# A chunked RWKV mixer on one core: the diagonal-block inverse moved ahead of the projection of v, state accumulators in two PSUM banks, two masks moved to VectorE

## The chip, the cores and the metric

The kernel runs on one core of one Trainium2 chip, as one launch. The metric is the device time of the whole launch in microseconds (us), as the median of several runs. Five engines work side by side: TensorE (PE: matmuls, and PEld: its weight loads), VectorE (DVE), ScalarE (ACT), GpSimd (POOL) and SyncE (SP, which here only issues DMAs). Matmul results land in PSUM, which has eight banks; everything else lies in SBUF.

## The reference

The program is a small two-part model over 256 tokens of width 1024. The part that the change touches is the "even mixer" of the second block: eight RWKV-7 heads of 64 channels, beside a multi-scale pooling branch.

```
S_t = S_{t-1} (diag(w_t) + a_t b_t^T) + v_t k_t^T ;  y_t = S_t r_t      (per head)
a = -kk,  b = kk * sigmoid(...),  kk = normalised k
y   = groupnorm(y);  bonus = sum(r * k * r_k) * v
o   = concat[(y + bonus) * g,  multiscale_pool(u_pool)] @ w_out
```

After this mixer comes a mixture of experts (32 experts, two per token), then an odd mixer (differential attention and S5 groups), and a second mixture of experts. Each expert has three weight matrices (gate, up, down) of 2 MB or 1 MB pieces, and they are read from HBM.

## The kernel before

`rwkv()` computes the recurrence in four chunks of 64 tokens. Heads are packed in pairs, so there are four pairs `p` and four chunks `b`, sixteen units of 128 partitions by 64. The work runs in these stages, which the prediction names:

- **Projections.** `shifted()` makes k, r and v: per tile of 128 channels, 24 matmuls of 128x256 (high and low parts of weight and input, L1203 to L1205 in the profile of before), then VectorE's `up` (L1208) and its combination (L1210). After r come four matmuls with `selT` (L1287), and VectorE makes the decayed factors: `AR` (a·decay and r·decay, L1295 and L1304), `sq` (the bonus product, L1313), `bb` (L1299) and `kb` (L1301). Then the projection of v; then the bonus product on PE (L1322), the gate product (L1327), transposes of v (L1333), and the pooling projection (L334 to L336, whose weights are split by VectorE in L326) with its small products.
- **Diagonal blocks.** Per pair, `diag()` multiplies `bb` with `AR` (64x128 per unit: the left half gives the matrix to invert, `Lr`, the right half an output factor, `ArbT`). ScalarE evicts `Lr` (L1429). VectorE masks it to 16x16 blocks (L1432 to L1437) and inverts these by forward substitution, 28 small instructions in a chain (L1441, L1443). Transposes and copies give `Tt` and `Tn`. `early` (L1385) are the factors that are scaled across chunks, for the products between different chunks, `offd()`.
- **State and outputs (the R stage).** Per pair: `diag` and `offd` of `kb`, masks (`lk`, L1474; `ark`, L1417), evictions (L1422, L1424), then the products into the accumulators R and Y, which stay open in PSUM. All these products have the helper's line, L1397.
- **Merging.** The 16x16 inverses become 32x32 (`mo1`) and 64x64 (`mo2`): GpSimd masks `Lr` (L1497), PE multiplies, and ScalarE and VectorE evict.
- **Recursion over the four chunks**, group norm, output projection, routing logits.

In PSUM, banks are handed out from named rings: "x" with six buffers and "w" with two. A scheduler orders the instructions of each engine; the code constrains it by `after()` and by priorities. Tiles come from pools, and a pool's space is used again when it is closed.

The weights of the experts come through a ring of eleven slots of 2 MB, w0 to w10, issued in a fixed order on SP's queue and, for two of the first loads, on GpSimd's. A slot may lie over mixer tiles, and its first load then waits until these are no longer read. The functions that the change touches are shown here.

Of the kernel before, what the change touches and what calls it, by code (L numbers as in the profile page):

```python
# [10 lines left out]
F32 = mybir.dt.float32  # L11
# [133 lines left out]
class K:  # L145
# [998 lines left out]
    def rwkv(self, keep):  # L1144
        nc, A, P, sh = self.nc, self.A, self.P, self.sh
        X = lambda shape: self.bank("x", shape, 6)
# [13 lines left out]
        V = keep.tile([128, 16, 64], F32, name="V")  # L1160
        opool = keep.tile([128, 4, T], F32, name="opool", tag="opool")
# [18 lines left out]
                                   gain=P("mix_g0"), bank="x", nb=6)  # L1180
# [118 lines left out]
        nc.vector.tensor_mul(bb, u16(kk), Ei)  # L1299
        with self.after(kkr):  # L1300
            nc.vector.tensor_mul(kb, u16(k), Ei)  # L1301
# [70 lines left out]
        zz, ux, u4, x1 = (whi(n, i) for i, n in enumerate(("zz", "ux", "u4", "x1")))  # L1372
# [5 lines left out]
        Lc, Ld = (zz[:, 512 * i:512 * i + 512].rearrange("p (u t) -> p u t", u=16) for i in range(2))  # L1378
        Ut = ux[:, 0:512].rearrange("p (u t) -> p u t", u=16)
        Uc, Z = (ux[:, 512 + 256 * i:768 + 256 * i].rearrange("p (u t) -> p u t", u=16) for i in range(2))  # L1380
        pd = lko1[:, 768:1024].rearrange("p (a b) -> p a b", a=16)
        Us, X1s = ([a[:, 512 * i:512 * i + 512].rearrange("p (u t) -> p u t", u=8) for i in range(2)] for a in (u4, x1))
# [5 lines left out]
        HS = [slice(64 * h, 64 * h + 64) for h in range(2)]  # L1388
        Lr = wlo("Lr", 3).rearrange("p (a b) -> p a b", a=16)
# [3 lines left out]

        def mm2(o, lhsT, rhs, start=True, stop=True):

            for h in HS:
                r = nc.tensor.matmul(o[h], lhsT[h], rhs[h], start=start, stop=stop, skip_group_check=not (start and stop))  # L1397
            return r
# [15 lines left out]
        def diag_out(dst, q):  # L1414

            d = bass.AP(tensor=dst.tensor, offset=dst.offset, ap=[dst.ap[0], [T + 64, 4], [1, 64]])
            nc.vector.tensor_mul(d, q[:, :, 64:128], mk("incl", 4))  # L1417
# [14 lines left out]
        nc.vector.tensor_mul(Lc, Lr[:, :, 0:32], C("m16")[:, None, 0:32].to_broadcast([128, 16, 32]))  # L1432
# [824 lines left out]
```

## Time and profile before

| | us |
|---|---|
| median of 3 runs (lowest to highest) | 1562.63 (1562.36 to 1564.98) |
| profiled execution, its own time | 1568.15 |
| span of the profiled execution | 1566.5 |
| PE busy in the span | 1281.4 (82%) |
| VectorE, ScalarE, GpSimd busy | 608.2, 403.6, 197.5 |
| moved by DMA | 499.09 MB, 319 GB/s over the span |

The span runs from the first to the last instruction of one execution that the hardware profiler took. It is 1.65 us shorter than that execution's own time, and that own time is 5.5 us above the median of the unprofiled runs, so differences of stages are applied to the median.

### The profile page before, as it was taken

The page shows a single profiled execution, that of the slowest core. Times are in us where ns is not written, and L with a number is a line of the kernel's source. Part 1 is how long each engine was busy: PE and PEld are TensorE (multiplying, and loading weights), DVE is VectorE, ACT ScalarE, POOL GpSimd, SP SyncE. Part 2 cuts the span into 40 slices and gives each one's busy share as a digit, 9 for nine tenths or more (in the row PEclk, how much of TensorE's full clock was granted, in tenths as well). Part 3 has the DMA queues.
Part 4 walks back from the last instruction along what each step waited for, and adds up shares of the span by engine and source line. Part 5 has one row for each costly group of instructions (what it writes and reads, how often), then busy time and mean ns, then how long its engine had stood idle before and what let it go on. Part 6 is the DMA issues. An engine that isn't in the chain of part 4 may idle for free.

```text
span 1566.5 us, 32856 instructions
## 1 busy us (share of the span) xinstructions
PE 1281.4 (82%) x14522; PEld 929.6 (59%) x14522; DVE 608.2 (39%) x1433; ACT 403.6 (26%) x767; POOL 197.5 (13%) x294
## 2 busy tenths in 40 slices
PE   7999999999978788677678686987888666777786
PEld 6887788779877755453454433866755442643543
DVE  7687678779644312412011012867311000101011
ACT  5455545555432110010010011635110000000011
POOL 2200021000022000742442001023100000000000
PEclk9999999999999898688898799998899897999898
DMA  9544344454307899999999998478899999999996
GB/s 361 191 179 158 141 168 152 158 194 149 150 27 307 360 425 417 410 424 421 419 419 425 425 411 367 127 159 336 337 425 423 426 426 427 423 425 426 424 424 275
DMA packets 51372, 499.09 MB, mean 319 GB/s; under 512 B 9452, under 2 KB 16784, under 8 KB 20632
## 3 DMA queue, kind: packets, MB, share of 16 engines
q1 hardware_dynamic: 50648, 492.20, 77.7%
q0 software_dynamic: 288, 4.19, 0.6%
q8 instruction: 117, 1.92, 0.5%
q10 hardware_dynamic: 288, 0.52, 0.1%
q14 instruction: 31, 0.25, 0.0%
HBM read 494.86 MB, written 2.04 MB: 317 GB/s over the span
## 4 chain that ended last, share of the span: by engine, by line
DMA 33%; PE 14%; DVE 3%; issue 1%; ACT 1%; SPq 0%; ACTq 0%
DMA w<-in_moe_w_down_dram 17%; DMA w<-in_moe_w_up_dram 11%; PE mm L934 4%; PE mm L854 3%; DMA w<-in_moe_w_gate_dram 3%; DMA w<-in_odd_in_dram 2%; PE tp L843 1%; DMA w<-s5H 1%; PE pj L334 1%; PE pj L335 1%; PE pj L336 1%; PE acc L875 0%; SPq L1849 0%; DVE probs L2041 0%; DVE zq L2003 0%
## 5 line engine op out<-in xcount | busy, mean ns | idle before, releaser
L854 PE MATMUL mm<-w,xt 128*32 128x128 f32 x8192 | 302.3, 300 | 114.1 <-DMA w<-in_moe_w_up_dram 49.7
L854 PEld LDWEIGHTS mm<-w,xt 128*32 128x32 f32 x8192 | 255.5, 120 | 155.9 <-issue 86.7
L934 PE MATMUL mm<-w,hidT 128*32 128x512 f32 x896 | 194.0, 663 | 49.7 <-DMA w<-in_moe_w_down_dram 49.1
L858 DVE SCALAR_TENSOR_TENSOR hid<-hid,mm 128x128 f32<-128x128 f32 x64 | 18.3, 286 | 377.0 <-ACT hid L857 377.0
L326 DVE TENSOR_TENSOR wlo<-w,whi 128x1024 fp32r<-128x1024 f32 x116 | 143.2, 1238 | 48.5 <-ACT whi L325 47.6
L325 ACT ACTIVATE whi<-w 128x1024 fp32r<-128x1024 f32 x124 | 131.0, 1058 | 117.9 <-PE pj L336 88.9
L934 PEld LDWEIGHTS mm<-w,hidT 128*32 128x32 f32 x896 | 43.4, 118 | 161.0 <-issue 114.3
L334 PE MATMUL pj<-whi,hT 128*128 128x512 f32 x316 | 123.0, 402 | 11.3 <-ACT whi L325 9.6
L335 PE MATMUL pj<-wlo,hT 128*128 128x512 f32 x316 | 125.5, 401 | 0.0
L336 PE MATMUL pj<-whi,hT 128*128 128x512 f32 x316 | 122.9, 397 | 0.7 <-DVE hT L306 0.7
L868 DVE SCALAR_TENSOR_TENSOR y<-mm,slotsc,y 128x512 fp32r<-128x512 f32 x36 | 26.9, 750 | 192.7 <-ACT y L867 190.0
L867 ACT ACTIVATE y<-mm,slotsc 128x512 fp32r<-128x512 f32 x36 | 24.8, 688 | 271.2 <-PE mm L934 245.3
L857 ACT ACTIVATE hid<-mm 128x128 f32<-128x128 f32 x64 | 17.7, 277 | 277.8 <-PE mm L854 277.8
L843 PEld LDWEIGHTS tp<-ohs,x 128*128 128x128 f32 x512 | 67.2, 215 | 25.3 <-issue 18.3
L843 PE MATMUL tp<-ohs,x 128*128 128x128 f32 x512 | 70.5, 301 | 11.1 <-DVE ohs L795 11.1
L334 PEld LDWEIGHTS pj<-whi,hT 128*128 128x128 f32 x316 | 60.1, 191 | 24.9 <-ACT whi L325 9.6
L336 PEld LDWEIGHTS pj<-whi,hT 128*128 128x128 f32 x316 | 60.0, 190 | 13.5 <-DVE hT L306 1.1
L335 PEld LDWEIGHTS pj<-wlo,hT 128*128 128x128 f32 x316 | 60.1, 190 | 13.0 <-DVE wlo L326 0.8
L875 PE MATMUL acc<-y,ohT 128*128 128x512 f32 x144 | 49.0, 442 | 11.3 <-DVE y L868 5.6
L844 DVE TENSOR_TENSOR xt<-tp,pk 128x512 f32<-128x512 f32 x32 | 22.1, 691 | 87.6 <-PE tp L843 87.6
L862 ACT ACTIVATE hidT<-tp 128x128 f32<-128x128 f32 x64 | 17.7, 277 | 145.6 <-PE tp L861 145.6
L861 PE MATMUL tp<-pk,hid 128*128 128x128 f32 x64 | 21.9, 342 | 31.9 <-DVE hid L859 31.4
(715 smaller groups left out, 2001.1 us busy)
## 6 DMA issues: line engine op xcount, KB each, us to landing
w<-in_moe_w_gate_dram SPq DMA_DIRECT2D x64, 2048.0 KB, 30.5
w<-in_moe_w_up_dram SPq DMA_DIRECT2D x64, 2048.0 KB, 22.4
w<-in_moe_w_down_dram SPq DMA_DIRECT2D x54, 2048.0 KB, 27.7
w<-in_w_in_dram SPq DMA_DIRECT2D x14, 2048.0 KB, 7.8
w<-in_moe_w_down_dram SPq DMA_DIRECT2D x16, 1024.0 KB, 30.3
w<-in_w_out_dram SPq DMA_DIRECT2D x4, 2048.0 KB, 7.8
w<-in_w_ple_gate_dram SPq DMA_DIRECT2D x4, 2048.0 KB, 7.8
w<-in_even_in_dram SPq DMA_DIRECT2D x4, 2048.0 KB, 8.0
```

The costliest lines, as they stand in the source:

```text
L325: nc.scalar.activation(h, w[:, i:i + s], AF.Copy)
L326: (engine or nc.vector).tensor_sub(l, w[:, i:i + s], h.bitcast(F32))
L334: nc.tensor.matmul(out, ah, wh, start=start, stop=False)
L335: nc.tensor.matmul(out, ah, wl, start=False, stop=False)
L336: return nc.tensor.matmul(out, al, wh, start=False, stop=stop)
L843: nc.tensor.matmul(p[:, k], xk[t][:, 4 * h + k], ohs[:, t], start=t == 0, stop=t == 1)
L844: nc.vector.tensor_mul(xt[:, ks], p, R["g"][:, ks, None].to_broadcast([128, 4, 128]))
L854: nc.tensor.matmul(gu[32 * q:32 * q + 32, i], xt(k), w[:, k, 128 * q:128 * q + 128], start=k == 0, stop=k == 7)
L867: nc.scalar.activation(y[0][b][r], dn[r], AF.Copy, scale=sc[r, 0:1])
L868: nc.vector.scalar_tensor_tensor(y[1][b][r], dn[r], sc[r, 0:1], y[0][b][r].bitcast(F32), op0=ALU.mult, op1=ALU.subtract)
L875: self.nc.tensor.matmul(acc[t][b], ohT[r, t], y[i][b][r], start=start and i == 0, stop=stop and i == 1)
L934: nc.tensor.matmul(dn[32 * j:32 * j + 32], hT[j][:, k], wd[j][:, 4 * b + k], start=k == 0, stop=k == 3)
```

## The change

1. The "x" ring has four buffers, and a new ring "q" has two, used for `offd` of `kb` and the first half of the output projection.
2. The matrix to invert, `Lr`, is made by 32 small products (64x64) of `bb` with the left half of `AR`, right after `bb` and ahead of the projection of v in the code. The masks and the forward substitution follow there too. `Lr`, `zz`, `ux` and `pd` get tiles of their own in the pool `keep`; before they lay in tiles shared with weight halves. `Tn` moves to the pool `rw_main`.
3. The right halves (`ArbT`) are 64x64 products of their own, in the "w" ring, later, beside `offd` of `bb`.
4. The accumulators R lie in two banks of eight units instead of four banks of four.
5. The masks of `mo1` and `mo2` are made by VectorE, into two tiles, `u4` and `u5`, instead of by GpSimd into one tile used twice.

```diff
-        X = lambda shape: self.bank("x", shape, 6)
+        X = lambda shape: self.bank("x", shape, 4)
+        Q = lambda shape: self.bank("q", shape, 2)
...
+        for i in range(2):
+            q = X([128, 8, 64])
+            for u in range(8 * i, 8 * i + 8):
+                mm2(q[:, u % 8], bb[:, u], ar[:, u, 0])
+            nc.scalar.activation(Lr[:, 8 * i:8 * i + 8], q, AF.Copy)
+        nc.vector.tensor_mul(Lc, Lr[:, :, 0:32], C("m16")[:, None, 0:32].to_broadcast([128, 16, 32]))
...
+        for t in range(2, 16):
+            nc.vector.tensor_mul(pd[:, 0:t, 0:t], Z[:, 0:t, 0:t],
+                                 Uc[:, t, 0:t][:, None, :].to_broadcast([128, t, t]))
+            nc.vector.tensor_reduce(Z[:, 0:t, t], pd[:, 0:t, 0:t], axis=AX.X, op=ALU.add)
         with self.after(kkr):
             nc.vector.tensor_mul(kb, u16(k), Ei)
...
-        for p in range(4):
-            q = diag(p, bb, X)
-            us = slice(4 * p, 4 * p + 4)
-            nc.scalar.activation(Lr[:, us], q[:, :, 0:64], AF.Copy)
-            diag_out(ArbT[:, p], q)
...
+        for U, us in zip(Us, (slice(0, 8), slice(8, 16))):
+            nc.vector.tensor_mul(U, Lr[:, us], mk("mo1", 8))
         Tt = m.tile([128, 16, 64], F32, name="Tt", tag="Tt")
-        Tn = keep.tile([128, 16, 64], F32, name="Tn", tag="Tn")
+        Tn = m.tile([128, 16, 64], F32, name="Tn", tag="Tn")
...
         for p in range(4):
             offd_out(ArbT[:, p], LabO[:, p], offd(p, bb, X))
+            q = W([128, 4, 64])
+            for b in range(4):
+                mm2(q[:, b], bb[:, 4 * p + b], AR0[:, p, b, 1])
+            diag_out(ArbT[:, p], q)
...
-        Rb = [[X([128, 4, 64]) for _ in range(2)] for _ in range(2)]
-        R = lambda b, p: Rb[p // 2][b // 2][:, 2 * (b % 2) + p % 2]
+        Rb = [X([128, 8, 64]) for _ in range(2)]
+        R = lambda b, p: Rb[p // 2][:, 2 * b + p % 2]
...
-            offd_out(Ark, LkO, offd(p, kb))
+            offd_out(Ark, LkO, offd(p, kb, Q))
...
+        for U, us in zip(U2s, U8):
+            nc.vector.tensor_mul(U, Lr[:, us], mk("mo2", 8))
         for n in ("mo1", "mo2"):
-            for U, us in zip(Us, U8):
-                nc.gpsimd.tensor_mul(U, Lr[:, us], mk(n, 8))
-            for U, X1, us in zip(Us, X1s, U8):
+            for U, X1, us in zip(Us if n == "mo1" else U2s, X1s, U8):
                 prod(X1, U, Tn[:, us])
...
-        bk = ("x", [128, 512], 6)
-        op = self.out_proj(oT, [[bk, bk], [bk, bk]], split)
+        bk = [(n, [128, 512], k) for n, k in (("q", 2), ("x", 4))]
+        op = self.out_proj(oT, [[bk[0]] * 2, [bk[1]] * 2], split)
```

The scheduler turns this into another order on the engines. Lines of the changed kernel are 4 higher than before up to the new code, and 10 to 33 higher behind it; the helper of small products is L1309 there.

On PE, behind the projection of r, the kernel before goes from the four `selT` products straight into the projection of v (L1203 to L1205, 96 products):

```order
L1278 MATMUL w<-pk,kkn_y 8x128 x2
L1287 MATMUL x<-kkr,selT 128x256 x4
L1203 MATMUL x<-hT,whi 128x256 x2
L1204 MATMUL x<-hT,wlo 128x256
L1205 MATMUL x<-hT,whi 128x256
L1203 MATMUL x<-hT,whi 128x256
```

The changed kernel has this there:

```order
L1282 MATMUL w<-pk,kkn_y 8x128 x2
L1291 MATMUL x<-kkr,selT 128x256 x4
L1355 MATMUL w<-srk,sq 128x8 x8
L1360 MATMUL w<-w_2840,lr 128x512
L1309 MATMUL x<-AR_2930,bb 64x64 x32
L1207 MATMUL x<-hT,whi 128x256
```

The bonus product (L1322 before, L1355 now), which stood behind the projection of v, the first gate product (L1360) and the 32 new small products now stand ahead of it.

On VectorE, at the same place, the kernel before mixes the work for v and for the pooling weights into the factors:

```order
L1313 TENSOR_TENSOR sq<-r,k 128x1024
L1295 SCALAR_TENSOR_TENSOR AR_2930<-kk,Eg 128x16x64
L1208 TENSOR_TENSOR up_3012<-x,rstdb 128x256
L326 TENSOR_TENSOR wlo<-w_3625,whi 128x1024
L1208 TENSOR_TENSOR up_3013<-x,rstdb 128x256
L1298 TENSOR_TENSOR kk<-kk,ta 128x1024
L326 TENSOR_TENSOR wlo<-w_3625,whi 128x1024
L1210 SCALAR_TENSOR_TENSOR V<-up_3012,evc,V 128x256
L1210 SCALAR_TENSOR_TENSOR V<-up_3013,evc,V 128x256
L1299 TENSOR_TENSOR bb<-kk,G 128x1024
```

The changed kernel has the factors first, then the masks, and then the substitution (L1330, L1332):

```order
L1346 TENSOR_TENSOR sq<-r,k 128x1024
L1299 SCALAR_TENSOR_TENSOR AR_2930<-kk,Eg 128x16x64
L1302 TENSOR_TENSOR kk<-kk,ta 128x1024
L1357 COPY bon<-w 128x8
L1303 TENSOR_TENSOR bb<-kk,G 128x1024
L1357 COPY bon<-w 128x8
L1363 TENSOR_TENSOR P_2922<-w,w_2840 128x512
L1321 TENSOR_TENSOR zz<-Lr,evc 128x512
```

The two `up` instructions, the two weight splits and the two V instructions that stood between sq and bb now stand behind the masks, between the steps of the substitution; `bon` (L1357), which needs the bonus product, stands ahead of bb.

On PE, at the start of the R stage, the kernel before has one pair's products up to the first wait (`lk` and `early` are the masked and evicted products of `kb`):

```order
L1397 MATMUL w<-AR_2930,kb 64x128 x4
L1397 MATMUL w<-early,kb 64x384 x2
L1397 MATMUL x<-V,lk 64x64 x2
L1397 MATMUL w<-early,kb 64x256 x2
L1397 MATMUL w<-early,kb 64x128 x2
L1397 MATMUL x<-V,early 64x64 x2
```

The changed kernel has there:

```order
L1309 MATMUL w<-AR_2930,kb 64x128 x8
L1309 MATMUL q<-early,kb 64x384 x2
L1309 MATMUL q<-early,kb 64x256 x2
L1309 MATMUL w<-AR_2930,kb 64x128 x8
L1309 MATMUL q<-early,kb 64x128
L1309 MATMUL x<-V,lk 64x64 x2
```

The `offd` products of `kb` (64x384, 64x256, 64x128) go to the ring q, and those of the first two pairs' `diag` (64x128 x8, twice) stand ahead of the first product into R; the `offd` of the first pair stands earlier still, among the pooling products.

## Rows read from the trace of the kernel before

**Rows 1.** Windows of the span, with clock, DMA share and rate.

```profile
core 0: us, PE busy (x) PEld busy (x) DVE busy (x) ACT busy (x) POOL busy (x), PEclk, DMA share, GB/s
524.00:532.00 8.00, 8.00 (x190) 7.83 (x193) 2.38 (x7) 0.66 (x2) 0.00 (x0) 0.91 0.37 113
...
532.00:960.00 428.00, 321.93 (x5000) 201.19 (x4991) 73.99 (x273) 37.87 (x102) 97.42 (x224) 0.87 1.01 420
```

**Rows 2.** Timeline of SP's queue of weight loads, 405 to 536 us.

```profile
479.47 0.33 SPq L244 DMA_DIRECT2D w<-in_moe_w_gate_dram  x1
...
531.51 0.33 SPq L244 DMA_DIRECT2D w<-in_moe_w_gate_dram  x1
```

**Rows 3.** Waits of SP's queue, 400 to 560 us.

```profile
SPq L244 <- PE x L1397: 56.9, 1, 56.9
...
SPq L244 <- PE mm L854: 21.7, 8, 6.9
```

**Rows 4.** Timeline of PE around the projections.

```profile
365.20 0.48 PE L1239 MATMUL x<-lr,w 64*128 64x256 f32 x1 [0.51 <-ACT ld L1240]
...
380.62 2.35 PE L1287 MATMUL x<-kkr,selT 8*128 8x256 f32 x8 [0.62 <-DVE kkr L1280]
...
397.15 1.84 PE L1322 MATMUL w<-srk,sq 128*128 128x8 f32 x16
...
411.24 1.02 PE L1327 MATMUL w<-w,lr 128*128 128x512 f32 x2
```

**Rows 5.** Windows: v at either clock, then the R stage.

```profile
382.97:388.83 5.86, 5.86 (x28) 5.86 (x29) 5.86 (x9) 0.19 (x1) 0.00 (x0) 0.50 0.30 78
388.83:397.15 8.32, 8.32 (x70) 8.32 (x70) 8.32 (x11) 3.90 (x5) 0.00 (x0) 0.99 0.47 199
...
428.20:456.80 28.60, 23.18 (x380) 19.65 (x378) 14.94 (x47) 11.55 (x33) 0.66 (x1) 0.88 0.18 74
```

**Rows 6.** Timeline of VectorE, factors, masks and inverse.

```profile
389.02 1.21 DVE L1313 TENSOR_TENSOR sq<-r,k 128x1024 f32<-128x1024 f32 x1
...
396.16 1.21 DVE L1299 TENSOR_TENSOR bb<-kk,G 128x1024 f32<-128x1024 f32 x1
...
411.44 3.50 DVE L1385 TENSOR_TENSOR early<-AR,E 128x1536 f32<-128x1536 f32 x3 [2.22 <-PE x L336]
...
423.37 1.52 DVE L1432 TENSOR_TENSOR zz<-Lr,evc 128x512 f32<-128x512 f32 x1
424.81 0.68 DVE L1433 TENSOR_TENSOR zz<-Lr,evc 128x512 f32<-128x512 f32 x1
...
428.05 0.16 DVE L1441 TENSOR_TENSOR lko<-ux 128x4 f32<-128x4 f32 x1
...
436.83 0.42 DVE L1474 TENSOR_TENSOR lk<-w,evc 128x256 f32<-128x256 f32 x1 [1.32 <-PE w L1397]
...
437.92 0.39 DVE L1443 TENSOR_REDUCE ux<-lko 128x15 f32<-128x225 f32 x1
```

**Rows 7.** Timeline of PE, small products of the chunk stages.

```profile
415.31 1.53 PE L1397 MATMUL x<-AR,bb 64*64 64x128 f32 x24
...
423.63 4.09 PE L1397 MATMUL x<-early,bb 64*64 64x256 f32 x36
...
428.32 0.98 PE L1397 MATMUL x<-evc,V 64*64 64x64 f32 x27
...
432.15 0.33 PE L1397 MATMUL x<-V,lk 64*64 64x64 f32 x4 [1.59 <-DVE lk L1474]
...
443.15 0.33 PE L1397 MATMUL x<-V,lko 64*64 64x64 f32 x4 [3.56 <-ACT lko L1422]
...
458.23 2.08 PE L1397 MATMUL w<-x,Tt 64*64 64x64 f32 x64
```

**Rows 8.** Waits of PE, 411 to 480 us.

```profile
PE w L1397 <- POOL u L1497: 2.1, 1, 2.1
```

**Rows 9.** Timeline of GpSimd, one mask.

```profile
423.07 1.26 POOL L1497 TENSOR_TENSOR u<-Lr,evc 128x512 f32<-128x512 f32 x1 [1.67 <-ACT Lr L1429]
```

More of the change, by code (lines that the diff above doesn't have):

```diff
@@ L1160, in rwkv @@
         V = keep.tile([128, 16, 64], F32, name="V")
+        Lr = keep.tile([128, 16, 64], F32, name="Lr")
+        zz, ux = (keep.tile([128, 1024], F32, name=n) for n in ("zz", "ux"))
+        pd = keep.tile([128, 16, 16], F32, name="pd")
         opool = keep.tile([128, 4, T], F32, name="opool", tag="opool")
@@ L1299, in rwkv, with mm2 @@
         nc.vector.tensor_mul(bb, u16(kk), Ei)
+        HS = [slice(64 * h, 64 * h + 64) for h in range(2)]
+        def mm2(o, lhsT, rhs, start=True, stop=True):
+            for h in HS:
+                r = nc.tensor.matmul(o[h], lhsT[h], rhs[h], start=start, stop=stop, skip_group_check=not (start and stop))
+            return r
+        Lc, Ld = (zz[:, 512 * i:512 * i + 512].rearrange("p (u t) -> p u t", u=16) for i in range(2))
+        Ut = ux[:, 0:512].rearrange("p (u t) -> p u t", u=16)
+        Uc, Z = (ux[:, 512 + 256 * i:768 + 256 * i].rearrange("p (u t) -> p u t", u=16) for i in range(2))
+        for i in range(2):
[4 more added lines that the diff above has]
+        nc.vector.tensor_mul(Lc, Lr[:, :, 0:32], C("m16")[:, None, 0:32].to_broadcast([128, 16, 32]))
+        nc.vector.tensor_mul(Ld, Lr[:, :, 32:64], C("m16")[:, None, 32:64].to_broadcast([128, 16, 32]))
+        nc.vector.tensor_add(Lc, Lc, Ld)
+        nc.vector.transpose(Ut.rearrange("p t c -> p (t c)"),
+                            Lc.rearrange("p u (i t) -> p t u i", i=2))
+        nc.vector.tensor_add(Uc, Ut[:, :, 0:16], Ut[:, :, 16:32])
+        nc.gpsimd.tensor_copy(Z, C("eye16").rearrange("p (x t) -> p x t", x=16))
+        nc.vector.tensor_copy(Z[:, 0:1, 1], Uc[:, 1, 0:1])
+        for t in range(2, 16):
+            nc.vector.tensor_mul(pd[:, 0:t, 0:t], Z[:, 0:t, 0:t],
+                                 Uc[:, t, 0:t][:, None, :].to_broadcast([128, t, t]))
+            nc.vector.tensor_reduce(Z[:, 0:t, t], pd[:, 0:t, 0:t], axis=AX.X, op=ALU.add)
         with self.after(kkr):
@@ L1371, in rwkv @@
         wlo = lambda n, i, dt=F32: sh.tile([128, 1024], dt, name=n, tag=f"wlo{i}")
-        zz, ux, u4, x1 = (whi(n, i) for i, n in enumerate(("zz", "ux", "u4", "x1")))
+        u4, x1 = whi("u4", 2), whi("x1", 3)
+        u5 = wlo("u5", 3)
         lk_, lko1 = wlo("lk", 0), wlo("lko1", 1)
@@ L1377, in rwkv @@
         ark1 = wlo("ark", 2)
[L1378 to L1382, printed above, removed]
+        Us, U2s, X1s = ([a[:, 512 * i:512 * i + 512].rearrange("p (u t) -> p u t", u=8) for i in range(2)] for a in (u4, u5, x1))
         for b in range(3):
@@ L1538, in rwkv @@
             for h in range(2):
-                copy(h, Rs[:, hs[h]], Rb[h][b // 2][:, 2 * (b % 2):2 * (b % 2) + 2])
+                copy(h, Rs[:, hs[h]], Rb[h][:, 2 * b:2 * b + 2])
             q = [W([128, 2, 64]) for _ in range(2)]
```

32 lines of the change are left out of this document (7 added, 25 removed).

## The prediction

> **What bounds the kernel now.** I read the windows of the span first. From 532 to 960 us, the first mixture of experts, the sixteen DMA engines are busy all the time, at 420 GB/s, while PE has idle time [rows 1]: the expert weights set the pace there. So I looked for where the stream of weights is held up. It is held up to 479.47 us: SP's next load waits 56.9 us for a product of the mixer (L1397, the recursion), because its slot lies over a mixer tile [rows 2, 3]. From there the ring fills; then all eleven slots are full, and from 524 to 532 us the rate is 113 GB/s [rows 1]. It resumes at 531.51 us, when the first expert's gate products (L854) give a slot back [rows 2, 3]. These products need the routing, the routing needs the mixer's output, and behind 531.51 us the stream is one piece. So whatever the mixer's end gains or loses moves the end of the kernel by the same amount, and the chain through the mixer, 380 to 506 us, is what must be costed. The profiled execution is 1568.15 us with a span of 1566.5; the median is 1562.63, and I apply the shift to the median.
>
> In that chain PE works nearly without a break from 383 to 428 us; the stage behind it, 428.2 to 456.8 us, holds 23.18 us of PE work in 28.6 us at a mean clock of 0.88 [rows 5], with two idle times, 1.59 us for VectorE's mask and 3.56 us for ScalarE's eviction [rows 7]. VectorE spends 428.05 to 438.31 us on the substitution, 28 instructions of 0.16 to 0.39 us [rows 6], on the same queue as those masks. One more PE wait stands further down: 2.1 us for GpSimd's mask [rows 8].
>
> **The change part by part.** I follow it by landmarks, each before against after.
>
> *Four X buffers instead of six.* The trace shows PE waiting 0.51 us for ScalarE's eviction of an X bank with six [rows 4]. With four, such waits come earlier, in the decay and gate products and at the transposes of the input. Nothing shows their size; below nothing is excluded, since no product gets a bank earlier, and above I bound it by one such wait for each of the eight products, 4 us. I take 1.5 us, three such waits. So the products with selT, which end at 382.97 us [rows 4], end at 384.5.
>
> *Start of v.* Before, v follows selT at once. Now PE has the bonus product next, which needs sq. VectorE finishes sq at 390.23 us [rows 6], so after at 391.7: PE stands idle some 7 us. Then bonus (1.84 us at full clock) and gate product (1.02 us) [rows 4] take 2.9 us, or 5.7 at half clock, to 394.6 or 397.4 us. On VectorE bb now comes after AR, kk·ta and the first bon; three instructions of 1.2 us end at about 395.4, where they ended at 397.37 before with splits and v between them [rows 6]. The 32 products of 64x64 have no row of their own form ahead of v; 64 records of a merging product of that form last 2.08 us, 27 of v's centring 0.98 [rows 7], two records to a product, so the 32 take 2.0 to 2.3 us, twice that at half clock. v thus starts between 397.5 and 401 us; I take 399. That is 16 us later than before.
>
> *v and the pooling projection.* Before, the first 5.86 us of v ran at clock 0.50, that is 1.2 GHz, 28 records; the rest made 70 records in 8.32 us at 2.4 GHz [rows 5], 0.119 us each. 96 products at full clock are 11.4 us against 14.2: v ends near 410.5 us, 13.3 later than its 397.15. If the clock is still low at its start, up to 3 us more. Behind it the bonus product (1.84 us) has gone, so that the pooling projection, whose end was at 411.24 us [rows 4], ends near 422.6, 11.4 later.
>
> Here the Trainium skill speaks against the change: "TensorE: Matmul & The Clock Gate", section "HAM oscillation — how this bites in real kernels", says that waits between bursts of matmuls drop the array to half rate, and that the burst behind them begins cold. The trace agrees in kind: the clock was 0.50 in v's first part, behind the light 8-row products. By that rule the new idle time would cost v its first part again, and the sum would end 3 us later than mine. This is the second rival's mechanism below.
>
> *The substitution on VectorE.* ScalarE evicts Lr by about 399.7. The masks, transpose and first column take some 3.9 us, from the masks' start to the first step being 4.7 before, with one mask of 1.52 us that is 0.68 undisturbed [rows 6]. The steps took 10.3 us before, of which 1.32 us was a wait for PE and some 1.4 us four masks of the R stage in between [rows 6]; without these 7.5 us. Between them now stand v's four up and four V instructions (0.4 us each by the mask of the same 128x256 shape) and four splits of 128x1024, 1.13 us from start to start as sq [rows 6], less one up that comes ahead, 7.3 us, and the two mo2 masks, 1.4 us. Behind them three bonus and gate instructions of 128x512, two of the half masks and a transpose, 4.5 us. In sum 399.7 + 3.9 + 7.5 + 7.3 + 1.4 + 4.5 = 424.3 us is where early starts, against 411.44 [rows 6]. Its first third is done 1.75 us later, at 426.05. Early is so bound by VectorE, with PE some 2 us ahead of it. This is 12.9 us later than before.
>
> *Between chunks.* From 426.05 PE has, at rates of before: five offd groups (four of bb and the first of kb; 36 records of one form in 3.9 us, 12 records to a group, 1.35 us each [rows 7]), the rest of the pooling products 0.6 us, the right halves of diag 1.9 us (64 records of half the width; 24 whole ones take 1.46 us to the next row's start [rows 7]), and the centring of v, 1.9 us. Then the first kb groups, diag twice and offd once (0.86 + 1.35 + 0.86 us), stand ahead of the first product into R. It starts near 441 us, against 432.15 [rows 7].
>
> *R stage.* 28.6 us before, of which 5.2 us are the two waits of [rows 7], and by the mean clock of 0.88 (0.24 of the window at 1.2 GHz, 6.9 us [rows 5]) half-speed stretches cost 3.4 us; without them it is 20.0. Now masks and evictions of the first two pairs are ready before their products, no step of the substitution stands before a mask, and 3.1 us of diag and offd are already counted: four times 2.4 us of products into R and Y, and two more diag and offd groups of 2.25 us, 14.1 us, to 455.1. A wait left between, for ScalarE's evictions, would cost at most what one did before, 3.56 us. With mo1's first products partly inside, their end, where the next merging products begin, is near 457 us, where it was 458.23 [rows 7]: 1.2 us earlier.
>
> *Masks.* mo2's products waited 2.1 us for GpSimd [rows 8], one of whose masks takes 1.26 us [rows 9]. VectorE now makes them from Lr long before, at 0.69 us each: 2.1 us less. VectorE's first mask of zz took 1.52 us while that one ran, from 423.07 us, and the second 0.68 [rows 6, 9].
>
> That fits the Trainium skill, "SBUF — State Buffer", section "Who interferes with whom": a VectorE instruction with two SBUF inputs and a GpSimd instruction that reads SBUF hold each other up. By it, 0.8 us go away here, on VectorE alone.
>
> *The rest.* R in two banks changes no product count; the recursion's copies and products now share banks, between 0 and 0.5 us, I take 0.3. The clock may drop in the shorter stage behind R: 0 to 1.7 us (half of one of the two stretches that the 6.9 us make), I take 0.8.
>
> *Two loads earlier.* Lr, zz and pd, and so the end of the first two slots' covers, are free, by the order of the tiles' last readers, at about 459 us (GpSimd's copy of opool, ahead of the merging) and not at 479: two loads of 2 MB, 4.9 us each at 420 GB/s, start ahead of the recursion's end. I cost them at nothing: the ring is full at 524 us and stands until 531.51 us [rows 1, 2]. If the stream were not full there they would be worth up to 9.9 us.
>
> **Sum.** −1.2 (R stage's end, with all the delay ahead of it) −2.1 (mask) +0.3 (recursion) +0.8 (clock) = −2.2 us. 1562.63 − 2.2 = **1560.4 us**. The sum is a small difference of large terms: +13 us up to early, −4 in the products between chunks, −10 in the R stage.
>
> **The rivals.**
> 1. *The gap is hidden better.* If v starts by 397.5 us and VectorE's substitution is ended sooner (its first and last instructions are 0.16 and 0.39 us [rows 6], so a mean near 0.25, 7 us busy, and the rest is gaps that other work can fill), early starts 3.4 us sooner, at 421, PE-bound, and with no clock loss and the X waits at 0.5 us the sum is −2.2 − 3.4 − 0.8 − 1 = −7.4, 1555 us. For it: gaps between dependent steps. Against it: the pooling projection on PE ends only near 422.
> 2. *Slower: v starts cold and late.* PE stands idle 7 us ahead of the bonus product and works in pieces until bb; v's first part again at clock 0.50 costs 3 us, the small products at half clock 2 us more, and from early on the chain takes them one for one: −2.2 + 3 + 2 + 2 (one more wait for an eviction in the R stage) = +4.8, 1567.4 us. It decides from the point at which early's first third comes later than 428.3 us. For it: the clock row of v before [rows 5]. Against: 3 of the 5 us fall on PE while VectorE is behind PE by 2 us there.
> 3. *The two earlier loads count in full*: −2.2 − 9.9 = −12.1, 1550.5 us. Against it the full ring and the idle rate of 113 GB/s behind 524 us [rows 1].
> 4. *It does nothing here*: the chain through the mixer isn't what the stream waits for, and another load holds the first expert: 1562.6 us. Against it the L854 wait [rows 3].
>
> **How the numbers follow.** Forecast 0.48 with a range of its own from 1557 to 1563.6, rival 1 0.17, rival 2 0.20, rival 3 0.06, rival 4 0.09. A change under 0.2%, 3.1 us, is about what a measurement here can't tell from none. Of the forecast, some 0.18 lie more than 3.1 us below, so faster is 0.18 + 0.17 + 0.06 = 0.41; slower is 0.19, nearly all of rival 2; the same 0.40. The range from 1553.5 to 1567.5 leaves out rival 3, and the tails of rivals 1 and 2.
>
> **What would show it.** PE: an idle time of about 7 us ahead of the bonus product, behind selT; v starting near 399 and ending near 410.5; the clock there at 1.00 (right) or 0.50 (rival 2). VectorE: early near 424. PE: first R product near 441, last near 455, no wait above 1 us between them; no wait for GpSimd at mo2. SP: two loads near 459, and the stream resuming some 2 us ahead of 531.5, with the slow stretch behind 520 us still there; if it is gone, rival 3 holds. The prediction is wrong if the loss ahead of early differs from 13 us by more than the R stage can absorb, or if the R stage still waits for ScalarE's evictions.

## The result and the profile after

The changed kernel is slower: a median of 1573.06 us over five runs (1570.08 to 1576.65), beside 1562.72 us of the kernel before over five runs (1562.36 to 1564.98). The ratio is 1.0059, with a 95% interval from 1.0044 to 1.0075. That is +10.3 us by the medians, +9.2 by the ratio, where I had forecast −2.2; it is slower than rival 2, the slowest case that I had priced (1567.4 us).

The profiled execution of the changed kernel took 1576.65 us, 3.6 us above its median. The page of the profile begins so:

```profile
span 1575.0 us, 32979 instructions
...
PE 1284.9 (82%) x14586; PEld 936.9 (59%) x14586; DVE 605.3 (38%) x1437; ACT 403.0 (26%) x765; POOL 191.6 (12%) x290
```

The engines have almost the same busy time as before, so the time went into the order and the waits. The timeline of PE in the changed kernel has the landmarks of the prediction (a row is: start, us, instruction, and in brackets the idle time ahead of it and what released it):

```profile
344.50 0.88 PE L298 MATMUL x<-pk,x 128*128 128x128 f32 x6 [1.85 <-DVE x L638]
...
385.19 2.39 PE L1291 MATMUL x<-kkr,selT 8*128 8x256 f32 x8 [0.62 <-DVE kkr L1284]
...
394.86 3.59 PE L1355 MATMUL w<-srk,sq 128*128 128x8 f32 x16 [7.27 <-DVE sq L1346]
398.30 2.06 PE L1360 MATMUL w<-w,lr 128*128 128x512 f32 x2
400.28 3.62 PE L1309 MATMUL x<-AR,bb 64*64 64x64 f32 x64
403.83 0.39 PE L1207 MATMUL x<-hT,whi 128*128 128x256 f32 x1
...
427.49 0.40 PE L336 MATMUL x<-whi,hT 128*128 128x512 f32 x1
...
446.88 0.22 PE L1309 MATMUL x<-V,lk 64*64 64x64 f32 x1
...
463.26 2.03 PE L1309 MATMUL w<-x,Tt 64*64 64x64 f32 x63
467.15 2.08 PE L1309 MATMUL w<-Tn,u 64*64 64x64 f32 x64
469.07 0.67 PE L1309 MATMUL w<-Tt,x 64*64 64x64 f32 x15
...
472.20 2.83 PE L1309 MATMUL w<-Tt,x 64*64 64x64 f32 x49 [2.46 <-issue]
474.82 0.64 PE L1309 MATMUL w<-rsa,Tt 64*64 64x64 f32 x8
```

The reader sees the idle time of 7.27 us ahead of the bonus product (L1355), as forecast. Behind it the bonus product, the gate product and the 32 small products (two records each) take 9.0 us, from 394.86 to 403.83 without a gap; the bonus product alone took 1.84 us before [rows 4], here 3.59. Then the first R product at 446.88 us, mo1's second products (L1309, x and Tt) at 463.26, and a new wait of 2.46 us in mo2's last products that the profile calls issue: PE waits there for nothing that the profile shows. The wait for GpSimd's mask [rows 8] is gone. VectorE, in the same profile:

```profile
404.59 0.69 DVE L1321 TENSOR_TENSOR zz<-Lr,evc 128x512 f32<-128x512 f32 x1 [2.88 <-ACT Lr L1320]
...
427.93 3.50 DVE L1415 TENSOR_TENSOR early<-AR,E 128x1536 f32<-128x1536 f32 x3
```

Early, which started at 411.44 us before [rows 6], starts at 427.93. The windows of the changed kernel (columns as in rows 1) show the clock:

```profile
390.00:400.00 10.00, 5.14 (x18) 3.92 (x18) 8.59 (x13) 0.00 (x0) 1.90 (x2) 0.50 0.58 212
400.00:411.00 11.00, 11.00 (x124) 10.65 (x124) 6.79 (x16) 4.41 (x6) 0.00 (x0) 0.83 0.01 2
...
440.00:460.00 20.00, 20.00 (x403) 18.23 (x401) 5.57 (x13) 8.84 (x35) 0.00 (x0) 1.00 0.42 178
...
472.20:475.00 2.80, 2.80 (x53) 2.80 (x54) 0.69 (x1) 0.00 (x0) 0.00 (x0) 0.50 0.95 404
```

Behind the idle time the granted clock stays at 0.50, that is 1.2 GHz, until v starts near 404 us; from 404 to 408 us it is 1.00. From 440 to 460 us, with the R stage from 446.88 on, PE has no idle time at all and a clock of 1.00, where before the R stage had 23.18 us of work in 28.6 at 0.88 [rows 5]. The last row is the end of mo2, behind the issue wait: half clock again. On SP's queue of weight loads:

```profile
463.55 0.33 SPq L244 DMA_DIRECT2D w<-in_moe_w_gate_dram  x1
463.97 0.39 SPq L244 DMA_DIRECT2D w<-in_moe_w_up_dram  x1
...
523.38 14.24 SPq L244 DMA_DIRECT2D w<-in_moe_w_down_dram  x2
539.04 0.33 SPq L244 DMA_DIRECT2D w<-in_moe_w_gate_dram  x1
```

Two loads go out at 463.55, and the stream resumes at 539.04 us, 7.5 us later than at 531.51 [rows 2], while the two spans differ by 8.5: most of the loss lies ahead of this point.

**The kernel before, once more.** The profile behind the prediction is of an execution 5.4 us above its kernel's median. The unchanged kernel was profiled once more (e12_before_again, below); that execution took 1563.01 us, close to the median. From here on stages are compared with it. Its timeline of PE, then of VectorE, then of SP:

```profile
379.07 1.99 PE L1287 MATMUL x<-kkr,selT 8*128 8x256 f32 x8 [0.61 <-DVE kkr L1280]
...
427.71 0.33 PE L1397 MATMUL x<-V,lk 64*64 64x64 f32 x4 [1.60 <-DVE lk L1474]
...
453.65 2.08 PE L1397 MATMUL w<-x,Tt 64*64 64x64 f32 x64
...
463.93 0.44 PE L1397 MATMUL w<-rsa,Tt 64*64 64x64 f32 x8
```

```profile
407.00 3.50 DVE L1385 TENSOR_TENSOR early<-AR,E 128x1536 f32<-128x1536 f32 x3 [2.21 <-PE x L336]
```

```profile
526.53 0.33 SPq L244 DMA_DIRECT2D w<-in_moe_w_gate_dram  x1
```

Both timelines are laid on the eight transposes of the input (L298), which start at 340.14 us in this execution and at 340.75 in the changed kernel's. From there, stage by stage (us; the forecast stands against the profile that it was made on):

| stage, by start of its landmarks | before, again | after | difference | forecast difference |
|---|---|---|---|---|
| transposes to selT | 38.9 | 44.4 | +5.5 | +1.5 |
| selT to early | 27.9 | 42.7 | +14.8 | +11.4 |
| early to the first R product | 20.7 | 18.9 | −1.8 | −4.0 |
| first R product to mo1's second products | 25.9 | 16.4 | −9.6 | −10.1 |
| these to the recursion's first product | 10.3 | 11.6 | +1.3 | −1.3 |
| the recursion's first product to the resumed stream | 62.6 | 64.2 | +1.6 | +0.3 |
| sum | | | +11.8 (11.9 before rounding) | −2.2 |

### The profile page after: what moved, and what is told of

Read it like the earlier page. It is cut to its first block, busy times and chain, and to the rows that moved or that the text cites. A ratio compares the mean times of both kernels' runs of the same rounds, so it can differ in the third digit from the quotient of the medians.

```text
span 1575.0 us, 32979 instructions
## 1 busy us (share of the span) xinstructions
PE 1284.9 (82%) x14586; PEld 936.9 (59%) x14586; DVE 605.3 (38%) x1437; ACT 403.0 (26%) x765; POOL 191.6 (12%) x290
## 4 chain that ended last, share of the span: by engine, by line
DMA 31%; PE 16%; DVE 3%; issue 1%; ACT 1%; POOL 0%; SPq 0%; ACTq 0%; POOLq 0%
DMA w<-in_moe_w_up_dram 17%; DMA w<-in_moe_w_down_dram 9%; PE mm L934 4%; PE mm L854 4%; DMA w<-in_moe_w_gate_dram 3%; DMA w<-in_odd_in_dram 2%; PE pj L334 1%; PE pj L335 1%; PE tp L843 1%; PE pj L336 1%; PE mm L957 0%; PE acc L875 0%; DVE probs L2051 0%; PE tp L1975 0%; DVE omx L2053 0%
## 5 line engine op out<-in xcount | busy, mean ns | idle before, releaser
L854 PEld LDWEIGHTS mm<-w,xt 128*32 128x32 f32 x8192 | 258.7, 122 | 146.0 <-issue 72.0
L934 PE MATMUL mm<-w,hidT 128*32 128x512 f32 x896 | 189.1, 654 | 52.0 <-DMA w<-in_moe_w_down_dram 51.2
L334 PE MATMUL pj<-whi,hT 128*128 128x512 f32 x316 | 123.7, 404 | 11.4 <-ACT whi L325 9.7
L843 PEld LDWEIGHTS tp<-ohs,x 128*128 128x128 f32 x512 | 68.8, 219 | 28.6 <-issue 22.1
```

The lines of the kernel that those rows point to most:

```text
L334: nc.tensor.matmul(out, ah, wh, start=start, stop=False)
L843: nc.tensor.matmul(p[:, k], xk[t][:, 4 * h + k], ohs[:, t], start=t == 0, stop=t == 1)
L854: nc.tensor.matmul(gu[32 * q:32 * q + 32, i], xt(k), w[:, k, 128 * q:128 * q + 128], start=k == 0, stop=k == 7)
L934: nc.tensor.matmul(dn[32 * j:32 * j + 32], hT[j][:, k], wd[j][:, 4 * b + k], start=k == 0, stop=k == 3)
```

## The experiments

Three theories stood against each other when I saw the result. **A**: the x ring of four banks is too short, and its waits and the half clock behind them are the loss. **B**: the order is, with v late behind bonus, gate and small products. **C**: the two earlier loads disturb PE. All kernels but e3, e7, e10 and e12 are edits of the changed kernel. Each ratio is against the kernel before, run beside it on the same chip.

**e1_six_banks** gives the projections' products, decay, selT and v the two q banks as well: banks 1 to 4 from x, 5 and 6 from q, in turn.

```diff
+        def X6(shape):
+            i = self.six % 6
+            self.six += 1
+            return X(shape) if i < 4 else Q(shape)
...
-            ps = X([128, T])
+            ps = X6([128, T])
```

> The changed kernel, but the projections of the low-rank inputs, k, r, the decay products, selT and v take their PSUM banks in turn from the four of x and the two of q, as if there were six again; all else as changed. Theory A (the four-bank ring is the cause: PE's waits at the input's transposes and the tanh products drop its clock twice, and v's first bank comes only after the small products): selT some 4 to 5 us earlier than in the changed kernel, v right behind selT near 383 us, no idle time of 7 us, early near 414 instead of 427.9, and a time of 1553 to 1560 us. Rival B (VectorE's chain with the substitution in it is the bound whatever the banks are): early moves by at most the 5 us of selT, and the time is 1566 to 1570 us.

Measured: 1562.38 us, ratio 0.9995 [0.9985, 1.0005]. That is between the numbers of the two theories, nearer A: by the ratios it is 0.64%, or 10.0 us, faster than the changed kernel, so the whole loss is gone, but no gain appears. In its profile selT's products, then early:

```profile
381.38 1.12 PE L1296 MATMUL q<-kkr,selT 8*128 8x256 f32 x4 [0.62 <-DVE kkr L1289]
419.05 3.48 DVE L1420 TENSOR_TENSOR early<-AR,E 128x1536 f32<-128x1536 f32 x3
```

Early comes 8.9 us sooner than in the changed kernel. From selT to early it is 37.7 us, 5.0 less than there: half of v's products now stand ahead of the bonus product. But v waits for its first bank, and the issue wait stayed (waits of PE, of this kernel: us in total, times, longest):

```profile
PE q L1212 <- DVE kk L1297: 4.5, 1, 4.5
...
PE w L1314 <- issue: 2.0, 1, 2.0
```

**e2_late_loads** was to hold the two loads back by two one-column copies on ScalarE that read `zz` and `Lr` behind the recursion.

```diff
+            for i, t in enumerate((zz, Lr[:, 0])):
+                nc.scalar.activation(gn[1][:, i:i + 1], t[:, 0:1], AF.Copy)
```

> The changed kernel, with two one-column copies by ScalarE, of zz and of Lr into a scratch tile, at the end of the recursion, so that the two loads of expert weights over these tiles can't start at 463.5 us but only behind the recursion. Theory C (the two earlier loads hold up PE's instruction fetch: PE waited 2.46 us for issue in the merging, and its clock fell behind that): that wait goes, the recursion starts 2.5 to 4 us earlier, and the time is 1569 to 1571 us against 1573. Rival D (the fetch is late whatever the loads do, or the loads bring what the wait costs): no difference, 1573 us, or up to 5 us slower if the earlier loads count.

Measured: 1572.17 us, 1.0057 [1.0041, 1.0074]. The copies did not hold the loads (they still start at 462.22 and 462.64 us), so the run says nothing on C.

**e3_masks_alone** is the kernel before with nothing but the masks of mo1 and mo2 on VectorE, in a fifth tile.

```diff
+        u5 = m.tile([128, 1024], F32, name="u5")
...
+        for U, us in zip(Us, (slice(0, 8), slice(8, 16))):
+            nc.vector.tensor_mul(U, Lr[:, us], mk("mo1", 8))
...
+        for U, us in zip(U2s, U8):
+            nc.vector.tensor_mul(U, Lr[:, us], mk("mo2", 8))
...
-                nc.gpsimd.tensor_mul(U, Lr[:, us], mk(n, 8))
```

> The kernel before with only one part of the change: the masks of mo1 and mo2 on VectorE, those of mo2 in a tile of their own. If the 2.1 us wait of PE for GpSimd's mask is worth its full size: no such wait, and 1560 to 1561 us against 1562.7. Rival: VectorE's four masks (0.69 us each) stand ahead of the substitution and of the R stage's masks and take back 1 to 3 us: 1562 to 1564 us.

Measured: 1556.92 us, 0.9958 [0.9941, 0.9975], or −6.6 us: three times the 2.1 us that the wait was, and more than either side had expected. The R stage shows the rest; its window, in the kernel before again and then here:

```profile
424.00:440.00 16.00, 10.65 (x156) 8.40 (x154) 12.96 (x40) 6.20 (x16) 0.00 (x0) 0.85 0.29 123
```

```profile
424.00:440.00 16.00, 14.13 (x242) 11.26 (x237) 14.72 (x47) 7.61 (x24) 0.00 (x0) 1.00 0.39 166
```

With the masks in other places the scheduler also moved ScalarE's copies of Tt behind the evictions of `lko`. The wait of 3.6 us for `lko` (as in [rows 7]) is gone, waits of 1.6 us for `early` and 1.3 for `lk` remain, and with shorter idle times the clock stays at 1.00. Laid on the same point, the stream resumes 7.4 us sooner, of which I count 2.1 to the mask's wait and most of the rest to this stage: from the first R product to mo1's second products it takes 21.3 us here, from 428.41 to 449.70, for 25.9.

**e4_v_first** keeps four banks, and puts the small products and the substitution behind the last product of v.

```diff
+        wv_ = load(2)
...
+        for p in range(4):
+            with self.after(kkr):
+                shifted(wv_, p, 8 + p, v[:, p])
...
-                mm2(q[:, u % 8], bb[:, u], ar[:, u, 0])
+            with self.after(self.last_sh):
+                for u in range(8 * i, 8 * i + 8):
+                    mm2(q[:, u % 8], bb[:, u], ar[:, u, 0])
```

> The changed kernel with its four banks, but the 32 small products and the substitution put behind the projection of v on PE. Theory A, its second half (v behind the small products at half clock is a loss of its own): v starts near 388 us, early comes some 5 to 7 us earlier than 427.9, and the time is 1566 to 1569 us; the delay at selT of 5 us stays. Rival B (VectorE's chain from Lr to early is the bound, and Lr comes no sooner here): early near 427, 1572 to 1574 us.

Measured: 1569.01 us, 1.0039 [1.0026, 1.0051]. By the ratios that takes back 0.20%, a third of the loss, and its interval overlaps the changed kernel's; in the profiles the stretch from selT to early is 39.7 us for 42.7. PE's largest wait in this stretch is now v's first product, for a bank:

```profile
PE x L1207 <- DVE kk L1292: 4.5, 1, 4.5
```

The four selT products hold all four banks of the ring until VectorE has read them (kk, L1292); what stands ahead of that read is shown under e7.

**e5_held_loads** holds the loads with two one-column additions on VectorE that read `pd` and `Lr`, and SA of the recursion; nothing uses their result.

```diff
+        for i, t in enumerate((pd[:, 0], Lr[:, 0])):
+            nc.vector.tensor_add(gn[1][:, i:i + 1], t[:, 0:1], SA[:, 0, 0:1])
```

> The changed kernel with two one-column additions by VectorE, of pd and of Lr to the last state of the recursion, into a scratch tile: they need the recursion's last result, so the two loads over pd and Lr can only start behind it, as in the kernel before. (The copies of the run with late loads waited for nothing and held nothing: its loads still started at 462.) Theory C (the two earlier loads hold up PE's instruction fetch): PE's wait for issue of 1.7 to 2.5 us in the merging is gone, and the time is 1569 to 1571 us. Rival D (the wait is there whatever the loads do): the wait stays, 1572 to 1574 us.

Measured: 1568.01 us, 1.0028 [1.0016, 1.0040], 0.31% better than the changed kernel, some 4.8 us. The loads start at 481.82 us, and the merging has no issue wait (one of 0.3 us stands in the R stage). Windows of the merging, in the changed kernel and here:

```profile
460.00:475.00 15.00, 12.54 (x353) 12.29 (x351) 3.75 (x6) 4.41 (x7) 9.29 (x4) 0.90 0.70 280
```

```profile
460.00:475.00 15.00, 14.37 (x413) 13.53 (x411) 5.03 (x9) 6.43 (x12) 11.41 (x5) 1.00 0.01 3
```

So C is real: wait and half clock go with the loads. Every other stage of the table agrees with the changed kernel's within 0.4 us; this one, from mo1's second products to the recursion, takes 7.8 us for 11.6. What the wait is, the DMA queues suggest. Queue q8 carries PE's instructions, judged by its count: 118 packets for PE's 29,172 instructions. From 462.5 to 469.5 us (packets, MB, share of the engines) the changed kernel moves weights alone, and this kernel one packet of instructions:

```profile
q1 hardware_dynamic: 115, 1.88, 72.1%
```

```profile
q8 instruction: 1, 0.02, 1.1%
```

In the changed kernel none comes in these 7 us; over 455 to 482 us it has five, as the kernel before. Its next one falls in 468 to 470 us:

```profile
q8 instruction: 1, 0.02, 3.1%
```

More finely, it starts at 469.8 us, as PE's wait begins, and 8.0 us behind the packet before it; in e5 the same packet comes 4.5 us behind the one before. Counted in the traces, it comes when PE has started 5797 to 5825 instructions (matmuls and weight loads) in the five kernels that have the wait, and 5611 to 5626 in the nine profiles without it; in all five PE goes on 2.2 to 2.4 us after it. So PE stood for instructions that came late. That the weight packets held them up is inferred from the runs without the loads.

**e6_six_banks_v_first** is e1 with v's block, and the two factors that stood ahead of it, ahead of the small products in the code, as in e4, but without e4's constraint; the small products take the six banks too.

```diff
+        wv_ = load(2)
+        v = V.rearrange("p (a b) t -> p a (b t)", a=4)
+        for p in range(4):
+            with self.after(kkr):
+                shifted(wv_, p, 8 + p, v[:, p])
...
-            q = X([128, 8, 64])
+            q = X6([128, 8, 64])
```

> The run with six banks, with the small products and the substitution put behind v in the code, so that v's first bank is not one that selT or the small products hold; there PE waited 4.5 us for it. Theory A: v right behind selT with no wait, early near 413, the R stage without long waits, and 1553 to 1557 us. Rival B (VectorE's chain with the substitution is the bound): early no sooner than 418, 1560 to 1563 us.

Measured: 1560.24 us, 0.9982 [0.9972, 0.9991]. Against e4, also with v first, that is 0.57%, or 8.9 us, which is the price of the short ring and of e4's constraint together. Early starts at 413.95 us, where A had it, but the time is B's; an issue wait of 1.6 us remains.

**e7_four_banks_alone** is the kernel before with the x ring of four and R in two banks; the two banks saved are left unused.

```diff
-        X = lambda shape: self.bank("x", shape, 6)
+        X = lambda shape: self.bank("x", shape, 4)
...
-        Rb = [[X([128, 4, 64]) for _ in range(2)] for _ in range(2)]
-        R = lambda b, p: Rb[p // 2][b // 2][:, 2 * (b % 2) + p % 2]
+        Rb = [X([128, 8, 64]) for _ in range(2)]
+        R = lambda b, p: Rb[p // 2][:, 2 * b + p % 2]
```

> The kernel before with only the accumulators R in two banks and the x ring of four; two PSUM banks stay unused; all work and its order in the code as before. Theory A, first half (four banks for the projections cost 3 to 5 us at selT, and nothing gives it back): selT 3 to 5 us later, and 1565 to 1568 us. Rival: the delay at selT is taken back behind it, since VectorE is the later engine there: 1562 to 1564 us.

Measured: 1575.64 us, 1.0076 [1.0064, 1.0089]: +11.9 us, more than the whole change. Its waits of PE from 340 to 520 us, and windows of PE and all engines at v:

```profile
PE x L1397 <- DVE lk L1474: 4.8, 1, 4.8
PE x L1203 <- DVE kk L1288: 4.5, 1, 4.5
...
PE x L298 <- DVE x L638: 2.3, 2, 1.9
```

```profile
383.00:390.00 7.00, 2.50 (x12) 1.97 (x11) 7.00 (x11) 0.30 (x1) 0.00 (x0) 0.64 0.17 33
390.00:400.00 10.00, 10.00 (x66) 10.00 (x66) 8.75 (x10) 3.03 (x4) 0.00 (x0) 0.74 0.46 188
```

The same first window in the kernel before again is full, at full clock:

```profile
383.00:390.00 7.00, 7.00 (x61) 7.00 (x60) 7.00 (x11) 2.12 (x2) 0.00 (x0) 1.00 0.63 222
```

v's bank costs 4.5 us of waiting, and the clock falls with it. VectorE's timeline of this kernel shows why the bank is late:

```profile
382.18 0.40 DVE L1280 COPY kkr<-w 8x256 f32<-8x256 f32 x1
382.51 1.20 DVE L1301 TENSOR_TENSOR kb<-k,G 128x1024 f32<-128x1024 f32 x1
383.65 4.61 DVE L1073 TENSOR_TENSOR wlo<-w,whi 128x1024 fp32r<-128x1024 f32 x4
388.19 0.47 DVE L1210 SCALAR_TENSOR_TENSOR r<-up,evc,r 128x256 f32<-128x256 f32 x1
388.58 1.40 DVE L1288 TENSOR_TENSOR kk<-kk,x 128x256 f32<-128x256 f32 x4
```

Between the copy that selT waits for and the four kk that read its banks stand `kb`, four weight splits and one `r`, 6.1 us. With six banks two were free for v meanwhile. Early starts at 419.39 us, 11.4 us later by the transposes: the whole loss stands ahead of early, 2.6 us of it ahead of selT. The wait of 4.8 us for `lk` comes in place of the waits that the kernel before has in the R stage, which takes 24.4 us here for 25.9; so R in two banks has no visible part in the loss.

**e8_six_v_held** joins e6 with the held loads of e5 (the two additions shown there).

> The run with six banks and v first, with the two additions that hold the two loads of expert weights back until the recursion's end. Theory C: 2 to 3 us faster than without them, 1551 to 1554 us. Rival D: the same as without them; if the earlier loads bring something, slower.

Measured: 1557.72 us, 0.9962 [0.9950, 0.9973]. No issue wait is left. Against e6 the held loads bring 0.20%, 3.1 us, with intervals that just touch.

**e9_products_later** moves e8's small products behind the first gate product, and masks and substitution with them in the code, since PE waited 1.3 us for `bb` in e8.

```diff
...
+            with self.after(gm0):
+                for u in range(8 * i, 8 * i + 8):
```

> The run with six banks, v first and held loads, with the 32 small products put behind the first gate product on PE. There PE waited 1.3 us for bb, and its clock was low until about 401 us. If that small stall and the clock behind it are worth their size, and the substitution has room behind early: no wait for bb, 1555 to 1556.5 us against 1557.7. Rival: the substitution is late next, and lk or the merging wait for it: 1557 to 1560 us.

Measured: 1558.42 us, 0.9959 [0.9944, 0.9974], no different from e8. The wait for `bb` has gone, another has come, and early starts later (417.24 us):

```profile
PE w L1349 <- DVE bon L1346: 1.7, 1, 1.7
```

**e10_selT_in_q** is e7 with the four selT products in the two unused banks, two to a bank, so that v finds its x banks free.

```diff
-            q = X([128, 2, T])
+            if p % 2 == 0:
+                qs = self.bank("q", [128, 2, T], 2)
```

> The run with four banks alone (1575.6 us), with the four products of selT in two banks of a ring of their own, two to a bank, so that v's first banks don't wait for VectorE's readers of selT. If v's 4.5 us wait and its clock at half speed behind that make most of the 12 us: v behind selT without a wait, and 1566 to 1569 us. Rival (the waits ahead of selT and in the R stage make most of it): 1571 to 1575 us.

Measured: 1569.83 us, 1.0039 [1.0024, 1.0054], 5.8 us better than e7. The windows at v:

```profile
383.00:390.00 7.00, 5.92 (x43) 5.07 (x42) 6.10 (x8) 1.46 (x2) 0.00 (x0) 1.00 0.01 2
390.00:400.00 10.00, 10.00 (x76) 9.07 (x75) 10.00 (x17) 4.21 (x6) 0.00 (x0) 1.00 0.57 210
```

No bank wait and no half clock there, and from selT to early it is 30.2 us, for 36.8 in e7: by the ratios this one wait, with the clock behind it, is about half of what the short ring costs (their intervals allow a quarter to three quarters). What is left stands, in this profile, ahead of selT, 44.5 us from the transposes for 38.9 (3.0 of the 5.6 us are half-clock stretches that e7's execution didn't have), and in the R stage, 28.5 us for 25.9, with waits of 5.5 us for `lko` and 2.0 for `ark`.

**e11_masks_gpsimd** is e8 with the masks on GpSimd again.

```diff
-            nc.vector.tensor_mul(U, Lr[:, us], mk("mo1", 8))
-            nc.vector.tensor_mul(U, Lr[:, us], mk("mo2", 8))
+                nc.gpsimd.tensor_mul(U, Lr[:, us], mk(n, 8))
```

> The run with six banks, v first and held loads, with the masks of mo1 and mo2 on GpSimd again, in one tile used twice. If the masks are worth here what they were alone (6 us in the masks alone run): 1563 to 1565 us, that is, the inverse ahead of v is worth nothing by itself. Rival (the masks' wait of 2.1 us is all that is theirs here, since the R stage has lost its other waits): 1559 to 1561 us.

Measured: 1560.87 us, 0.9973 [0.9963, 0.9984]. The wait is back, as it was before:

```profile
PE w L1314 <- POOL u L1509: 2.2, 1, 2.2
```

Against e8 the masks are worth 0.11%, some 1.7 us; the intervals overlap, so the wait in the profile carries this more than the ratios do. Without them, the inverse ahead and R in two banks, with six banks and the loads held, gain 0.27%, 4.2 us.

**e12_before_again** is the kernel before, unchanged, profiled once more.

> The kernel before, unchanged, profiled once more. Its first profiled execution was 5.4 us over its median, and held v's first 5.86 us and two stretches of the R stage at clock 0.50; the masks alone run, whose instructions are the same up to early, had v at full clock and early 2.9 us sooner. If these half-speed stretches of the first profile are chance: here v's first part, or the R stage, or both are at full clock, and the profiled time is nearer to the median, 1560 to 1566 us. If they belong to the kernel: clock 0.50 behind selT and twice in the R stage again, and 1567 to 1569 us.

Measured: 1563.01 us in one execution, and 1563.02 in another beside it. What recurs in this second profile belongs to the kernel: the three waits of the R stage and the mask (1.6, 3.6 and 2.1 us) and half-clock stretches there. v's first part ran at 1.00 (the window shown under e7), where the first profile had 0.50 [rows 5]: that was of one execution.

## Why the prediction was wrong

**The step that failed first is "Four X buffers instead of six".** I costed it at 1.5 us, three waits of 0.51 us, and bounded it at 4, by the only wait for a bank in the trace. Alone it costs 11.9 us (e7), and the changed kernel gains 10.0 us when it gets six banks back and nothing else is edited (e1). The bound was wrong because the waits with six banks said nothing of those with four: selT's four banks are read behind 6.1 us of other work on VectorE's queue, and only with six banks could v start meanwhile. The place was wrong too, for I looked for the ring's price ahead of selT only. There, in the first row of the table, it is 5.5 us for 1.5: 2.6 as in e7, which has the same ring and no half clock there, and 2.9 of two half-clock stretches behind the wait of 1.85 us and near 370 us, for which the sum had no term. In the changed kernel itself v doesn't meet its bank wait, since the idle time for sq comes first. But with six banks half of v moves ahead of the bonus product, and selT to early falls from 42.7 to 37.7 us (e1): I had counted the late v as the price of the new order and not asked whether the ring made it late.

**Start of v: rival 2 in kind.** The idle time came as forecast (7.27 for some 7 us), and I had left the clock behind it open, 2.9 to 5.7 us for two products. It took the bad end for nearly all of them, the small products too: 9.0 us together, where I had taken 7.3 (391.7 to 399). With the bonus product already 3.2 us late by selT's delay, v started at 403.83 for 399; v itself then ran at clock 1.00. The Trainium skill, "TensorE: Matmul & The Clock Gate", section "HAM oscillation — how this bites in real kernels", has the rule that the burst behind a wait begins cold; the trace agrees, with 0.50 in the window of 390 to 400 us. Of rival 2's terms (+4.8 us) only the half clock ahead of v came true; the half clock in v's first part and the eviction wait in the R stage did not.

**selT to early.** I forecast 42.2 us for this stretch and it took 42.7, in part by luck: the products ahead of v took 1.7 us more, and VectorE's chain from zz's first mask to early 23.3 us, where I had 24.6. Its two sides were not as I said: PE was not 2 us ahead of VectorE. The pooling projection's last product stands at 427.49 us and early at 427.93. What failed is the base. I counted v's first 5.86 us at half clock, 2.9 us of loss, as something the change removes. In the second profile of the kernel before that loss isn't there (selT to early is 27.9 us, and 27.9 in e3, the same up to early), so the median held no such gain. It is 2.9 of the 3.4 us by which this row is off.

**Between chunks.** From early to R I forecast 16.7 us; it took 18.9, without idle time on PE. I had counted 0.6 us of the pooling branch's small products there. The pooling projection ended only at early's start, so all of them fell behind it: with the last transposes of v they take 3.2 us ahead of the first `offd` product (427.73 to 430.94 us), and the rest comes later.

**R stage: right.** 16.4 us to mo1's second products for a forecast of 16, no wait, clock 1.00. The change does what it says there, and it gives 9.6 us. But in e3 about half of that, 4.6 us, came from the moved masks and the order on ScalarE alone, so the gains of masks and inverse don't add: e8 with all of it (0.9962) is where e3 is (0.9958).

**Masks: right.** The wait of 2.1 us went; zz's first mask took 0.69 us where it had taken 1.52 [rows 6] beside GpSimd's (1.52 again in e12, and 0.68 in e3, whose masks are VectorE's), which is what "SBUF — State Buffer", section "Who interferes with whom", of the Trainium skill says.

**Two loads earlier: the sign was missing.** I put them at nothing, and the other case that I gave was a gain of 9.9 us. They cost 2.46 us of waiting and a half clock of 2.8 us (1.4 us) behind it; e5 and e8 get 4.8 and 3.1 us back without them. They were of no use, as forecast: the stream stands until the first expert's products, at 539.04 us with them and at 535.85 in e5 without.

**The sum.** By the sign that I had set it failed: the loss ahead of early is 20.3 us by the first two lines of the table, and 16.5 against the first profile, for 13, and the R stage absorbed no more than forecast. By the table the forecast is off by 14.0 us: 4.0 ring with its half clock, 3.4 v and base, 2.2 between chunks, 0.5 R stage, 2.6 loads and clock, 1.3 behind the recursion, where I know no cause (by the same landmarks e3, e6 and e8 differ from e12 too, by up to 2). In medians it is 12.5; the profiled execution of the changed kernel was itself 3.6 us above its median, about what its two half-clock stretches at the projections cost. Of the six kernels with four banks, e5 and e10 show these stretches too and e2, e4 and e7 don't, so how much of the 2.9 us the median holds is open.

Five versions beat both kernels: e3 (0.9958), e9 (0.9959), e8 (0.9962), e11 (0.9973) and e6 (0.9982). The intervals of the first three nearly coincide; which is best is open, and e3 is by far the smallest edit.

## What to carry to other kernels

Before a ring of PSUM banks is cut, list for each bank the instruction that frees it and what stands ahead of that instruction on its own engine; here the waits seen with the longer ring gave no bound. Then ask what the scheduler will put elsewhere because a bank is missing. Price an idle time of PE on the main chain twice, as the wait and, as a risk, as the half clock behind it, and a load that a change releases earlier as a possible cost to whatever runs beside it. Before a stretch of a single profiled execution enters a sum, see how far that execution stands from the median, and take a second profile if there is one to be had.

## What the runs showed of the hardware

The granted clock differs between executions for the same instructions and the same waits. v's first part in the kernel before had 0.50 in one execution and 1.00 in another, 2.9 us apart. Behind the same wait of 1.85 us at the transposes, the changed kernel and e7 had (PE alone: us, busy, clock, DMA share, GB/s):

```profile
346.00:348.00 2.00, 2.00 (x9) 0.50 0.00 1
```

```profile
346.00:348.00 2.00, 1.72 (x14) 1.00 0.03 12
```

e5 and e10 show 0.50 in this window as well, e2 and e4 1.00. A short wait was so a risk of half clock here and not a fixed price. The other surprise is the issue wait: with two weight loads in flight during the merging PE stood for 1.6 to 2.5 us in five kernels (2.46 in the changed one, 2.0 in e1 and e4, 1.7 in e2, 1.6 in e6), and not at all in the merging of e5, e8, e9 and e11, which held the loads. Under e5 it is shown that in those five kernels a packet of PE's instructions came late, and that PE went on 2.2 to 2.4 us after it.
